# A three-pass feed-forward product with two token halves in one moving operand, and a join of smaller edits, in a one-core network kernel

## The chip, the cores and the metric

The kernel runs on one core of one Trainium2 chip. The metric is the device time of one execution in microseconds (us); the figure for a kernel is the median of several runs. A separate execution was taken by the hardware profiler; all rows below come from that one execution.

## The reference, cut to what matters

There are 256 tokens of width 1024, all in 32-bit floating point. The network is two blocks in a row:

```
h = x + 0.5 * rms_norm(swiglu(rms_norm(x), w_gate, w_up, w_down))      # ffn1
h = h + rms_norm(hybrid_mixer(rms_norm(h)) @ w_out)                    # mix
h = h + rms_norm(memory_cross_attention(rms_norm(h), rms_norm(mem)))   # mem
h = h + 0.5 * rms_norm(swiglu(rms_norm(h), ...))                       # ffn2
# second block, modulated by c @ w_ada + b_ada (six rows of 1024)
h = h + g1 * (conformer_conv + gated differential attention) @ w_out   # blk
h = h + g2 * mixture of 64 experts(norm(h))                            # moe

def swiglu(x, w_gate, w_up, w_down):
    return (silu(x @ w_gate) * (x @ w_up)) @ w_down                    # 1024 -> 2816 -> 1024
```

## The kernel before, in words

The stages ffn1, mix, mem, ffn2, blk and moe follow one another; each reads and updates the residual `h`, kept in the on-chip memory (SBUF) as two token tiles t = 0 and t = 1 of 128 tokens.

**Precision.** Most products are done in three passes. `split` (L178) cuts an operand into a high part `hi` (a cast by ACT to a 32-bit matmul type) and a low part `lo` (the rest, a subtraction on DVE); a product is hi·hi + hi·lo + lo·hi, three matmuls into one accumulator (`mm3`, L388; `lin_feat`, L573). Weights arrive from HBM in granules of 512 KB (`gran`, L294; four buffers `wraw`) and are split into `whi` and `wlo` (four buffers each).

**Feed-forward.** `ffn` (L527) does the first 512 of the 2816 inner columns in token-major form (`lin_tok2`, L434: the token slice is the stationary operand, 512 weight columns stream), and the remaining 2304 in nine blocks of 256 columns in feature-major form (`lin_feat`: a 128x128 weight block is stationary, all 256 tokens stream). In such a block each of the two matrices takes 8 slices of the inner dimension times 2 column groups times 3 matmuls:

```
583  nc.tensor.matmul(p, hi, xh[:, k], start=k == 0, stop=False)
584  nc.tensor.matmul(p, hi, xl[:, k], start=False, stop=False)
585  mm = nc.tensor.matmul(p, lo, xh[:, k], start=False, stop=k == K - 1)
```

After both matrices ACT takes silu of the gate sum out of the accumulator, DVE multiplies by the up sum, and the result is split into `hh`, `hl` (L554 to L558). The down projection (`lin_wide`, L464) uses token slices of these as stationary operands; its last eight slices are kept back and done for t = 0 first and then for t = 1, so that t = 0 is complete while t = 1 still runs.

**Between stages.** `post_norm` (L276) and `norm_T` (L226) finish the residual and make the next stage's normalised input: sums of squares on ACT, a power on POOL, products on DVE and POOL, then `trans` (L265), which transposes 4 slices at a time on the tensor engine (L186) and splits the result into two tensors `xTh` and `xTl` (`xT`, L193). For t = 0 the transposes come in program order, behind all matmuls of the stage before; for t = 1 they are kept in `second` and issued by `mid` (L254) behind a given matmul, the end of the first product's work on t = 0.

**Work hung between.** `tick` (L355) counts granules, and `at(n, f)` issues `f` at a later count. The modulation rows run this way inside the feed-forwards: 48 rounds of a DVE multiply-add of a 512 KB weight tile into `aacc` (L1337), and for each of the six rows `ada_end` (L1341), two matmuls with 32 columns of ones, a copy, and a store of one row to DRAM. Vectors that are wanted in all 128 partitions are loaded by `bcast` (L171) from one row in HBM; vectors that are wanted as columns go through `cols` (L588), a load of rows and a transpose.

Each engine does its instructions in the order in which the scheduler put them at build time; `issue_after(i)` places instructions behind `i` in the order of their engine. DMAs of weights are issued on SP's queue.

Of the kernel before, what the change touches and what calls it, by code (L numbers as in the profile page):

```python
# [26 lines left out]
CNORM = 1  # L27
# [92 lines left out]

def _freqs():
    import numpy as np

    return np.power(500000.0, -np.arange(0, 16, 2) / 16.0).astype(np.float32)[None]


class Net:


    def __init__(self, tc, A, es):  # L130
        self.tc, self.nc, self.A, self.es = tc, tc.nc, A, es
        pool = lambda name, bufs, **k: es.enter_context(tc.tile_pool(name=name, bufs=bufs, **k))
        self.cst = pool("cst", 1)
        self.wraw = pool("wraw", NRAW)
        self.whi = pool("whi", 4)
        self.wlo = pool("wlo", 4)
        self.act = pool("act", 1)
        self.ps = pool("ps", 8, space=PSUM)
        nc = self.nc
# [9 lines left out]
        self.now, self.todo, self.second, self.late = 0, [], [], []  # L149
        self.steady = {}  # L150
        self.tags, self.xp, self.half, self.xi, self.hold = None, None, None, 0, None
# [19 lines left out]
    def bcast(self, vec, n=D, tag="gB", bufs=3, eng=None):  # L171

        t = self.act.tile([P, n], F32, name=tag, tag=tag, bufs=bufs)
        (eng or self.nc.sync).dma_start(t, vec.broadcast_to([P, n]))
        return t
# [4 lines left out]
    def transpose_split(self, src, hi, lo, t, full=None):  # L180

        nc = self.nc
        n = src.shape[-1] // P
        pt = self.psum("tp")
        for c in range(n):
            nc.tensor.transpose(pt[:, c * P : (c + 1) * P], src[:, c * P : (c + 1) * P], self.ident)  # L186
        pv = pt[:, : n * P].rearrange("p (c t) -> p c t", c=n)
        sl = slice(t * P, (t + 1) * P)
        self.split(hi[:, :, sl], lo[:, :, sl], pv)
        if full is not None:  # L190
            self.nc.scalar.copy(full[:, :, sl], pv)

    def xT(self, tag="xT", bufs=1, kc=8):  # L193
# [32 lines left out]
    def norm_T(self, src, gain, pre=None, out=None, late=False):  # L226


        nc = self.nc
        gB = self.bcast(gain)  # L230
        hi, lo = out or self.xT()

        def tile(t):
            if pre is not None:
                pre(t)
            x = self.halves(src, t)
            rs = self.sumsq(x)
# [3 lines left out]
            nc.vector.tensor_scalar(xn[1], xn[1], rs, None, ALU.mult)  # L241
            for b in range(2):
                self.trans(xn[b], hi, lo, b, t)

        tile(0)
# [19 lines left out]
    def trans(self, xn, hi, lo, b, t, full=None):  # L265

        def tr():
            o = slice(4 * b, 4 * b + 4)
            self.transpose_split(xn, hi[:, o], lo[:, o], t, full if full is None else full[:, o])

        if t == 0:
            tr()
        else:
            self.second.append(tr)
# [19 lines left out]
    def gran(self, ap, eng=None, more=None):  # L294

        nc = self.nc
        kc, n = ap.shape[0] // P, ap.shape[1]
        raw = self.raw([P, kc, n])
        self.loaded = nc.sync.dma_start(raw, ap.rearrange("(c p) n -> p c n", p=P))
        return self.wsplit(raw, eng, more)  # L300

    def raw(self, shape):
# [6 lines left out]
        if tag != "wraw":  # L309

            if self.half is None:
                if tag == "xT":
                    self.xi = 1 - self.xi
                    x = self.act.tile([P, 2, 1024], F32, name="wx", tag="xTh" if self.xi else "xTl", bufs=1)
                else:
                    x = self.mp.tile([P, 2, 1024], F32, name="wx", tag=tag, bufs=LB)
# [117 lines left out]
    def lin_tok2(self, xT, blocks, more, done=None):  # L434
# [10 lines left out]
        for t in range(2):  # L445
            for i, ((W, c0, n, ps), hl) in enumerate(zip(blocks, ws)):
                for k, w in enumerate(hl):
                    x = [v[:, k, t * P : (t + 1) * P] for v in xT]
                    mm = self.mm3(ps[t][:, :n], x, w, k == 0, k == len(hl) - 1)
                    if t and k % 2:  # L450
                        self.tick(mm)
                if t and done is not None:
                    done(i)
            if t == 0:
                self.mid(mm)
# [8 lines left out]
    def lin_wide(self, xT, W, last=True, first=False, bias=None, ws=None, ps=None, more=None):  # L464
# [8 lines left out]
        def go(t, ws, n):  # L473
            for i, (k, hl) in enumerate(ws):
# [5 lines left out]
                if n and i % n == n - 1:  # L480
                    self.tick(mm)
            return mm

        k = 0
        while k < K:
# [7 lines left out]
            for t in range(2):  # L493
                mm = go(t, w, 2 if n > 1 else t)
                if k == t == 0:
                    self.mid(mm)
# [18 lines left out]
    def load_x(self):  # L515
# [3 lines left out]
        self.nc.sync.dma_start(self.ident, self.A["consts"][:, :P])  # L519

        def pre(t):
            if t == 1:
                self.nc.sync.dma_start(self.h[:, 1], x[:, 1])
# [3 lines left out]
    def ffn(self, n, pre=None, ada=()):  # L527
# [3 lines left out]
        with self.tc.tile_pool(name="ffn", bufs=1) as pool:  # L531
# [56 lines left out]
    def cols(self, rows, n, name="cols", dst=None, at=None, tag="ds"):  # L588

        nc = self.nc  # L590
        if at is None:
            r = self.act.tile([n, P], F32, name="rowsT", tag="rowsT", bufs=2)
        else:
            r = self.mp.tile([n, P], F32, name="rowsT", tag=tag, bufs={"ds": 3, "daT": 2}[tag])
        nc.sync.dma_start(r, rows)
        o = dst if dst is not None else self.mp.tile([P, n], F32, name=name)

        def turn():
            pt = self.psum("tp")
            nc.tensor.transpose(pt[:, :n], r, self.ident[:n, :n])  # L600
            nc.vector.tensor_copy(o, pt[:, :n])

        if at is None:
            turn()
        else:
            self.at(at, turn)
        return o
# [66 lines left out]
    def mixer_consts(self, mp):  # L674
# [10 lines left out]
        def loads():  # L685
# [5 lines left out]
            nc.sync.dma_start(gnB, A["gdn_out_norm"].broadcast_to([P, P]))  # L691
            for a, b, n in ((0, 1536, 8), (8, 3592, 8)):
# [5 lines left out]
        def tables():  # L698
            self.cols(A["gdn_conv_w"][0].rearrange("i (c p) -> (i c) p", p=P), 48, dst=cw)
# [610 lines left out]
    def ada_start(self):  # L1310
# [3 lines left out]
        self.modr = [dr.tile([1, D], F32, name="modr%d" % i) for i in range(6)]  # L1314
# [3 lines left out]
        def start():  # L1318
            self.cols(A["c_2"].rearrange("o (c p) -> (o c) p", p=P), 8, dst=self.cc)
# [21 lines left out]
    def ada_end(self, i, acc):  # L1341

        nc = self.nc
        ps = self.psum("ada")
        for b in range(2):
            nc.tensor.matmul(ps[32 * b : 32 * b + 32], self.ones[:, :32], acc[:, b * 512 : b * 512 + 512],
                             start=True, stop=True)
        r = self.mp.tile([P, 512], F32, name="ar", tag="s", bufs=3)[:64]
        nc.scalar.copy(r, ps[:64])
        for b in range(2):  # L1350
            nc.sync.dma_start(self.modr[i][:, b * 512 : b * 512 + 512], r[32 * b : 32 * b + 1])
# [26 lines left out]
    def norm_mod_T(self, gain, i, pre):  # L1378
# [6 lines left out]
        for t in range(2):  # L1385
# [76 lines left out]
    def conv_consts(self):  # L1462
        A = self.A
        row = lambda n: A[n].rearrange("o (c p) -> (o c) p", p=P)
        self.lng = self.cols(row("conv_ln_g_2"), 8, "lng", at=5, tag="daT")
        self.lnb = self.cols(row("conv_ln_b_2"), 8, "lnb", at=6, tag="daT")
        dw = A["conv_dw_2"][0].rearrange("i (c p) -> (i c) p", p=P)
        return [self.cols(dw[0:128], 128, "dw0", at=2), self.cols(dw[128:248], 120, "dw1", at=3),
                self.cols(row("conv_dw_b_2"), 8, "bdw", at=4)]
# [364 lines left out]
    def moe_norm(self, pre, each):  # L1834
# [4 lines left out]
        xf = self.act.tile([P, 8, T], F32, name="xf", tag="xTl", bufs=1)  # L1839
# [550 lines left out]
c_2 positions_2 w_ada_2 b_ada_2 norm1_g_2 w_in_2 conv_dw_2 conv_dw_b_2 conv_ln_g_2 conv_ln_b_2 w_pw2_2  # L2390
# [27 lines left out]
```

## Time and profile before

| What | Value |
|---|---|
| median of 3 runs | 1421.91 us (1420.5 to 1423.75) |
| the profiled execution's own time | 1420.49 us |
| its span, first to last instruction | 1418.7 us |
| PE (matmuls) busy | 1365.4 us, 96% |
| DVE busy | 902.9 us, 64% |
| ACT busy | 670.2 us, 47% |
| mean granted clock of the tensor engine | 0.995 of full |

PE is the tensor engine, DVE, ACT and POOL are the vector, scalar and general engines, SP issues the DMAs. Matmuls are pipelined: the duration in a row of PE contains the passage through the array, and what a matmul costs in a stream is the distance from one start to the next.

### The profile page before, as it was taken

The page shows a single profiled execution, that of the slowest core. Times are in us where ns is not written, and L with a number is a line of the kernel's source. Part 1 is how long each engine was busy: PE and PEld are TensorE (multiplying, and loading weights), DVE is VectorE, ACT ScalarE, POOL GpSimd, SP SyncE. Part 2 cuts the span into 40 slices and gives each one's busy share as a digit, 9 for nine tenths or more (in the row PEclk, how much of TensorE's full clock was granted, in tenths as well). Part 3 has the DMA queues.
Part 4 walks back from the last instruction along what each step waited for, and adds up shares of the span by engine and source line. Part 5 has one row for each costly group of instructions (what it writes and reads, how often), then busy time and mean ns, then how long its engine had stood idle before and what let it go on. Part 6 is the DMA issues. An engine that isn't in the chain of part 4 may idle for free.

```text
span 1418.7 us, 23583 instructions
## 1 busy us (share of the span) xinstructions
PE 1365.4 (96%) x8901; PEld 1068.5 (75%) x8901; DVE 902.9 (64%) x1419; ACT 670.2 (47%) x1055; POOL 127.5 (9%) x111
## 2 busy tenths in 40 slices
PE   6999999999999999999999989999999999999996
PEld 4999878889777879998798768675456566657662
DVE  5878567864457598664669997767226555555452
ACT  5544555634346454444453465943115444444440
POOL 1000012110101020000200313123000000000000
PEclk9999999999999999999999999999999999999999
DMA  8889666343245278875677534467889999999996
GB/s 283 272 291 321 208 197 211 102 137 107 75 158 180 94 262 303 280 241 182 199 242 214 168 119 134 134 209 280 336 317 409 408 408 354 409 408 409 365 409 260
DMA packets 148788, 358.00 MB, mean 252 GB/s; under 512 B 16099, under 2 KB 53931, under 8 KB 148671
## 3 DMA queue, kind: packets, MB, share of 16 engines
q1 hardware_dynamic: 148671, 356.46, 70.7%
q8 instruction: 71, 1.16, 0.3%
q14 instruction: 46, 0.38, 0.1%
HBM read 354.81 MB, written 1.60 MB: 251 GB/s over the span
## 4 chain that ended last, share of the span: by engine, by line
PE 44%; DMA 9%; DVE 7%; ACT 2%; issue 1%; POOL 0%; SPq 0%; DVEq 0%; ACTq 0%; POOLq 0%
DMA wx<-in_exp_gu 5%; PE eg L2209 4%; PE gx L2052 3%; DMA wx<-in_w_exp_down 3%; PE y L2220 2%; DVE wlo L178 2%; PE lw L393 2%; PE lw L392 2%; PE lw L391 2%; PE eg L2161 1%; PE eg L2160 1%; PE u L583 1%; PE g L584 1%; PE g L583 1%; PE u L585 1%
## 5 line engine op out<-in xcount | busy, mean ns | idle before, releaser
L178 DVE TENSOR_TENSOR wlo<-wraw,whi 128x1024 fp32r<-128x1024 f32 x248 | 308.9, 1253 | 137.5 <-ACT whi L178 135.6
L178 ACT CAST whi<-wraw 128x1024 fp32r<-128x1024 f32 x250 | 260.7, 1049 | 244.2 <-PE lw L393 50.1
L178 DVE TENSOR_TENSOR wlo<-wx,whi 128x1024 fp32r<-128x1024 f32 x76 | 89.8, 1221 | 18.7 <-ACT whi L178 17.7
L2209 PE MATMUL eg<-wx,xe 128*32 128x512 f32 (+1 forms) x480 | 84.1, 595 | 0.7 <-DMA wx<-in_exp_gu 0.7
L583 PE MATMUL u<-xTh,whi 128*128 128x256 f32 x288 | 82.2, 285 | 0.0
L583 PE MATMUL g<-xTh,whi 128*128 128x256 f32 x288 | 81.6, 283 | 0.0
L584 PE MATMUL g<-xTl,whi 128*128 128x256 f32 x288 | 81.5, 283 | 0.0
L585 PE MATMUL g<-xTh,wlo 128*128 128x256 f32 x288 | 81.5, 283 | 0.0
L585 PE MATMUL u<-xTh,wlo 128*128 128x256 f32 x288 | 81.5, 283 | 0.0
L584 PE MATMUL u<-xTl,whi 128*128 128x256 f32 x288 | 81.5, 283 | 0.0
L178 ACT CAST whi<-wx 128x1024 fp32r<-128x1024 f32 x76 | 77.0, 1050 | 8.0 <-DMA wx<-in_exp_gu 4.8
L2111 DVE SCALAR_TENSOR_TENSOR es<-es,gsl,eg 128x256 f32<-128x256 f32 (+2 forms) x27 | 13.0, 480 | 90.0 <-ACT es L2110 90.0
L1337 DVE SCALAR_TENSOR_TENSOR aacc<-wada,cc,aacc 128x1024 f32<-128x1024 f32 x48 | 61.5, 1282 | 9.9 <-DMA wada<-in_w_ada 9.5
L178 DVE TENSOR_TENSOR yl<-y,yh 128x512 fp32r<-128x512 f32 (+2 forms) x54 | 36.6, 688 | 43.8 <-ACT yh L178 43.8
L2110 ACT ACTIVATE es<-eg 128x256 f32<-128x256 f32 (+2 forms) x27 | 10.4, 384 | 111.2 <-PE eg L2209 90.8
L2209 PEld LDWEIGHTS eg<-wx,xe 128*32 128x32 f32 (+1 forms) x480 | 22.5, 116 | 48.3 <-issue 40.7
L2052 PE MATMUL gx<-G,h2h 128*128 128x256 f32 (+1 forms) x240 | 58.3, 285 | 0.0
L583 PEld LDWEIGHTS u<-xTh,whi 128*128 128x128 f32 x288 | 55.2, 192 | 3.4 <-ACT sf L556 3.4
L393 PE MATMUL lw<-whi,hl 128*128 128x512 f32 x144 | 56.8, 394 | 0.0
L391 PE MATMUL lw<-whi,hh 128*128 128x512 f32 x144 | 56.6, 393 | 0.0
L392 PE MATMUL lw<-wlo,hh 128*128 128x512 f32 x144 | 56.6, 393 | 0.0
L2052 PE MATMUL gx<-G,h2l 128*128 128x256 f32 (+1 forms) x240 | 56.6, 278 | 0.0
(698 smaller groups left out, 3689.9 us busy)
## 6 DMA issues: line engine op xcount, KB each, us to landing
wx<-in_exp_gu SPq DMA_DIRECT2D x172, 512.0 KB
wraw<-in_w_in SPq DMA_DIRECT2D x84, 512.0 KB
wx<-in_w_exp_down SPq DMA_DIRECT2D x84, 512.0 KB
wada<-in_w_ada SPq DMA_DIRECT2D x48, 512.0 KB
wraw<-in_ffn_w_gate SPq DMA_DIRECT2D x44, 512.0 KB
wraw<-in_ffn_w_up SPq DMA_DIRECT2D x44, 512.0 KB
wraw<-in_ffn_w_down SPq DMA_DIRECT2D x44, 512.0 KB
wraw<-in_exp_gu SPq DMA_DIRECT2D x40, 512.0 KB
```

The lines of the kernel that those rows point to most:

```text
L178: return self.nc.scalar.copy(hi, src), (eng or self.nc.vector).tensor_sub(lo, src, hi.bitcast(F32))
L391: nc.tensor.matmul(o, x[0], w[0], start=start, stop=False)
L392: nc.tensor.matmul(o, x[0], w[1], start=False, stop=False)
L393: return nc.tensor.matmul(o, x[1], w[0], start=False, stop=stop)
L583: nc.tensor.matmul(p, hi, xh[:, k], start=k == 0, stop=False)
L584: nc.tensor.matmul(p, hi, xl[:, k], start=False, stop=False)
L585: mm = nc.tensor.matmul(p, lo, xh[:, k], start=False, stop=k == K - 1)
L1337: nc.vector.scalar_tensor_tensor(acc, w, self.cc[:, k : k + 1], acc, ALU.mult, ALU.add)
L2052: nc.tensor.matmul(ps[:, i * n : (i + 1) * n], h[:, t, f], G[:, t], start=j == 0, stop=j == 3)
L2160: nc.tensor.matmul(ps, xh[:, c], hi, start=c == 0, stop=False)
L2209: mm = nc.tensor.matmul(ps[o], xe[:, k, o], w[k // 2][:, k % 2], start=k == 0, stop=k == 7)
L2220: mm = nc.tensor.matmul(y[o], hT[:, c, o], w[4 + c][:, 0, b * 512 : b * 512 + 512], start=c == 0, stop=c == 1)
```

## The change

Everything stands in one diff:

- In the nine feed-forward blocks `lin_feat2` takes the place of `lin_feat`. High and low token parts lie side by side, so that one matmul per high weight block streams 512 columns (high tokens into the left half of the accumulator, low tokens into the right), and the low weight block streams the 256 high columns into the left half. ACT then copies the right half out and DVE adds the left half to it, for gate and up, before the silu.
- The normalised input is held in two tiles of four slices each, with high and low inside a slice (`Half` gives the old view of it).
- `lin_wide` notes the matmul that ends its last slice but one for t = 1 (`gap`); the next stage's transposes for t = 0 are issued right behind it, at a raised priority. `mid` is called one or two slices earlier than before.
- In ffn1 the splits of the first four gate granules are placed behind steps of the first token tile's norm (`turns`). 18 matmuls of ones by ones are issued at the start (`WARM`). The first load of `x` is followed by the gain, then by the identity.
- Gains, the modulation rows and several column vectors lie in HBM already spread over 128 partitions or as columns; `cols` and its transposes go. `ada_end` does two matmuls with all 128 columns of ones and stores 128 rows.
- In the block's norm the product of the first half with the gain moves from POOL to DVE.

```diff
+class Half:
+    def __getitem__(self, key):
+        p, k, *rest = key
+        j = (k.start if type(k) is slice else k) // 4
+        k = slice(k.start - 4 * j, k.stop - 4 * j) if type(k) is slice else k - 4 * j
+        return self.tiles[j][(p, k, self.i, *rest)]
...
     def xT(self, tag="xT", bufs=1, kc=8):
-        hi = self.act.tile([P, kc, T], F32R, name=tag + "h", tag=tag + "h", bufs=bufs)
-        lo = self.act.tile([P, kc, T], F32R, name=tag + "l", tag=tag + "l", bufs=bufs)
-        return hi, lo
+        self.xw = [self.act.tile([P, kc // 2, 2, T], F32R, name=tag, tag=tag, bufs=2 * bufs) for _ in range(2)]
+        return [Half(self.xw, i) for i in range(2)]
...
+            self.turns = [first[0], first[1], first[1], first[2]]
...
         if t == 0:
-            tr()
+            with ExitStack() as es:
+                if self.gap is not None:
+                    es.enter_context(self.tc.issue_after(self.gap.ins))
+                    es.enter_context(self.tc.high_priority(offset=GAP))
+                done = tr()
...
+                if i == len(ws) - 2:
+                    if t and last and ws[-1][0] == K - 1:
+                        self.gap = mm
+                    if t == ws[0][0] == 0:
+                        self.mid(mm)
...
+        for _ in range(WARM):
+            self.nc.tensor.matmul(ps[:, :P], self.ones, self.ones, start=True, stop=True)
...
-                g, u = [self.psum_feat(n, FW // P) for n in "gu"]
-                self.lin_feat(xT, wg, c0, g)
-                self.lin_feat(xT, wu, c0, u)
+                g, u = [[self.psum(n) for _ in range(FW // P)] for n in "gu"]
+                self.lin_feat2(self.xw, wg, c0, g)
+                self.lin_feat2(self.xw, wu, c0, u)
                 for m in range(FW // P):
-                    s = pool.tile([P, T], F32, name="sf", tag="sf", bufs=4)
-                    nc.scalar.activation(s, g[m], AF.Silu)
-                    nc.vector.tensor_mul(s, s, u[m])
+                    s, v = [pool.tile([P, T], F32, name="sf", tag="sf", bufs=6) for _ in range(2)]
+                    for o, p in ((s, g[m]), (v, u[m])):
+                        nc.scalar.copy(o, p[:, T:])
+                        nc.vector.tensor_add(o, p[:, :T], o)
+                    nc.scalar.activation(s, s, AF.Silu)
+                    nc.vector.tensor_mul(s, s, v)
...
+    def lin_feat2(self, xw, W, c0, ps):
+                    both = lambda: nc.tensor.matmul(p.rearrange("p (i t) -> p i t", i=2), hi, xw[k // 4][:, k % 4],
+                                                    start=k == 0, stop=k == K - 1)
+                    if k < K - 1:
+                        both()
+                    mm = nc.tensor.matmul(p[:, :T], lo, xw[k // 4][:, k % 4, 0], start=False, stop=False)
+                    if k == K - 1:
+                        mm = both()
...
     def ada_end(self, i, acc):
-        ps = self.psum("ada")
         for b in range(2):
-            nc.tensor.matmul(ps[32 * b : 32 * b + 32], self.ones[:, :32], acc[:, b * 512 : b * 512 + 512],
-                             start=True, stop=True)
...
+            ps = self.psum("ada")
+            nc.tensor.matmul(ps, self.ones, acc[:, o], start=True, stop=True)
...
-                nc.gpsimd.tensor_mul(xn, x[b], gB[:, s])
+                (nc.gpsimd if b else nc.vector).tensor_mul(xn, x[b], gB[:, s])
```

## Rows read from the trace of the kernel before

**Rows 1.** The page: busy us (share) xcount; PE busy tenths in 40 slices.
```profile
PE 1365.4 (96%) x8901; PEld 1068.5 (75%) x8901; DVE 902.9 (64%) x1419; ACT 670.2 (47%) x1055; POOL 127.5 (9%) x111
...
PE   6999999999999999999999989999999999999996
```
**Rows 2.** Timeline of PE, one gate-and-up block: start us, us, instruction.
```profile
52.87 0.28 PE L583 MATMUL g<-xTh,whi 128*128 128x256 f32 x1
...
64.39 0.28 PE L583 MATMUL g<-xTh,whi 128*128 128x256 f32 x1
```
**Rows 3.** Timelines of PE and DVE, end of ffn1, start of mix.
```profile
203.63 0.40 PE L393 MATMUL lw<-whi,hl 128*128 128x512 f32 x1
...
206.97 0.48 DVE L241 TENSOR_SCALAR xn<-xn,rs 128x512 f32<-128x512 f32 x1
...
208.66 0.39 PE L391 MATMUL lw<-wmore,hh 128*128 128x512 f32 x1
...
210.03 1.04 PE L186 MATMUL tp<-ident,xn 128*128 128x128 f32 x8
211.54 0.50 PE L391 MATMUL fv<-whi,xTh 128*128 128x512 f32 x1 [0.47 <-ACT xTh L178]
```
**Rows 4.** The page, costliest groups: busy us, mean ns of one, idle before.
```profile
L557 DVE TENSOR_TENSOR sf<-sf,u 128x256 f32<-128x256 f32 x36 | 13.8, 418 | 2.2 <-PE u L585 2.2
```
**Rows 5.** Windows in the feed-forward blocks: busy us per engine, clock, DMA, GB/s.
```profile
52.90:145.00 92.10, 92.10 (x757) 89.97 (x756) 73.30 (x85) 43.53 (x66) 0.95 (x1) 1.00 0.91 309
...
532.50:626.70 94.20, 94.20 (x781) 93.18 (x781) 70.59 (x82) 42.98 (x64) 0.96 (x1) 1.00 0.86 285
```
**Rows 6.** Waits of DVE, 52.9 to 145: us in total, times, longest.
```profile
DVE wlo L178 <- ACT whi L178: 13.5, 16, 2.0
DVE aacc L1337 <- DMA wada<-in_w_ada: 2.4, 6, 0.6
```
**Rows 7.** Timeline of all engines, the first 28 us.
```profile
4.08 0.63 ACT L211 ACTIVATE junk<-h 128x512 f32<-128x512 f32 x1 [1.75 <-DMA h<-in_x]
...
8.87 1.26 POOL L239 TENSOR_TENSOR xn<-h,gB 128x512 f32<-128x512 f32 x1 [2.41 <-DMA gB<-in_ffn_pre_norm]
10.15 1.04 ACT L178 CAST whi<-wraw 128x1024 fp32r<-128x1024 f32 x1 [4.59 <-DMA wraw<-in_ffn_w_gate]
11.23 1.23 DVE L178 TENSOR_TENSOR wlo<-wraw,whi 128x1024 fp32r<-128x1024 f32 x1 [5.47 <-ACT whi L178]
11.49 1.04 ACT L178 CAST whi<-wraw 128x1024 fp32r<-128x1024 f32 x1 [0.30 <-DMA wraw<-in_ffn_w_gate]
12.37 0.75 DVE L240 SCALAR_TENSOR_TENSOR xn<-h,rs,gB 128x512 f32<-128x512 f32 x1
...
13.17 1.97 PE L186 MATMUL tp<-ident,xn 128*128 128x128 f32 x8 [13.17 <-DVE xn L240]
...
14.96 0.80 PE L391 MATMUL g<-whi,xTh 128*128 128x512 f32 x1
...
27.70 1.03 PE L186 MATMUL tp<-ident,xn 128*128 128x128 f32 x8
```
**Rows 8.** Waits of PE, whole span: us in total, times, longest.
```profile
PE lw L393 <- DVE xTl L178: 1.5, 1, 1.5
...
PE lw L391 <- ACT xTh L178: 1.0, 2, 0.8
```
**Rows 9.** Window of the block's join, columns as in rows 5.
```profile
940.00:946.00 6.00, 4.26 (x11) 3.16 (x12) 4.69 (x7) 0.72 (x2) 1.50 (x3) 0.72 0.79 223
```
**Rows 10.** Timelines and one group of PE: modulation row, whole-width plain 32-bit product, column transposes.
```profile
140.90 1.05 PE L1346 MATMUL ada<-aacc,ones 128*32 128x512 f32 x4
141.88 0.38 PE L583 MATMUL u<-xTh,whi 128*128 128x256 f32 x1
...
978.23 5.37 PE L2011 MATMUL sh<-wraw,xf 128*128 128x512 f32 x12
...
L600 PE MATMUL tp<-ident,rowsT x7: 222/225/272, 40.2 to 732.4; 8*128 8x8 f32 x4, 48*128 48x48 f32 x1, 128*128 128x128 f32 x1, 120*128 120x120 f32 x1
```

More of the change, by code (lines that the diff above doesn't have):

```diff
@@ L147, in __init__ @@
         self.h = self.cst.tile([P, 2, D], F32, name="h")
-        self.now, self.todo, self.second, self.late = 0, [], [], []
+        self.now, self.todo, self.second, self.late, self.turns, self.gap = 0, [], [], [], [], None
         self.steady = {}
-        self.tags, self.xp, self.half, self.xi, self.hold = None, None, None, 0, None
+        self.tags, self.xp, self.half, self.hold = None, None, None, None
     def low(self, n):
@@ L240, in tile @@
             nc.vector.scalar_tensor_tensor(xn[0], x[0], rs, gB[:, :512], ALU.mult, ALU.mult)
[L241 to L245, printed above, removed]
+            done = nc.vector.tensor_scalar(xn[1], xn[1], rs, None, ALU.mult)
+            return [(done,)] + [self.trans(xn[b], hi, lo, b, t) for b in range(2)]
+        first = tile(0)
         if late:
+            self.turns = [first[0], first[1], first[1], first[2]]
             self.late.append(lambda: tile(1))
@@ L268, in tr @@
             o = slice(4 * b, 4 * b + 4)
-            self.transpose_split(xn, hi[:, o], lo[:, o], t, full if full is None else full[:, o])
+            return self.transpose_split(xn, hi[:, o], lo[:, o], t, full if full is None else full[:, o])
         if t == 0:
-            tr()
-        else:
-            self.second.append(tr)
+            with ExitStack() as es:
[3 more added lines that the diff above has]
+                done = tr()
+            if b == 1:
+                self.gap = None
+            return done
+        self.second.append(tr)
     def post_norm(self, fps, gain, mul):
@@ L299, in gran @@
         self.loaded = nc.sync.dma_start(raw, ap.rearrange("(c p) n -> p c n", p=P))
-        return self.wsplit(raw, eng, more)
+        with ExitStack() as es:
+            for i in self.turns.pop(0) if self.turns else ():
+                es.enter_context(self.tc.issue_after(i.ins))
+            return self.wsplit(raw, eng, more)
     def raw(self, shape):
@@ L311, in raw @@
             if self.half is None:
[L312 to L316, printed above, removed]
+                pool, bufs = (self.act, 2) if tag == "xT" else (self.mp, LB)
+                x = pool.tile([P, 2, 1024], F32, name="wx", tag=tag, bufs=bufs)
                 self.half = x[:, 1]
@@ L586, in lin_feat @@
             self.tick(mm)
-    def cols(self, rows, n, name="cols", dst=None, at=None, tag="ds"):
+    def lin_feat2(self, xw, W, c0, ps):
         nc = self.nc
[L591 to L607, printed above, removed]
+        K, n = W.shape[0] // P, len(ps) * P
+        kc = 1024 // n
+        for k0 in range(0, K, kc):
+            for k, w in enumerate(self.gran(W[k0 * P : (k0 + kc) * P, c0 : c0 + n]), k0):
+                for m, p in enumerate(ps):
+                    hi, lo = [v[:, m * P : (m + 1) * P] for v in w]
+                    both = lambda: nc.tensor.matmul(p.rearrange("p (i t) -> p i t", i=2), hi, xw[k // 4][:, k % 4],
[5 more added lines that the diff above has]
+                        mm = both()
+            self.tick(mm)
     def b4(self, name, dtype=F32):
@@ L1313, in ada_start @@
         dr = self.es.enter_context(self.tc.tile_pool(name="dram", bufs=1, space=bass.MemoryType.DRAM))
-        self.modr = [dr.tile([1, D], F32, name="modr%d" % i) for i in range(6)]
+        self.modr = [dr.tile([P, D], F32, name="modr%d" % i) for i in range(6)]
         self.ud = [dr.tile([P, 2 * (T + 3)], F32, name="ud%d" % i) for i in range(2)]
@@ L1343, in ada_end @@
         nc = self.nc
-        ps = self.psum("ada")
         for b in range(2):
-            nc.tensor.matmul(ps[32 * b : 32 * b + 32], self.ones[:, :32], acc[:, b * 512 : b * 512 + 512],
-                             start=True, stop=True)
[L1348 to L1351, printed above, removed]
+            o = slice(b * 512, b * 512 + 512)
+            ps = self.psum("ada")
+            nc.tensor.matmul(ps, self.ones, acc[:, o], start=True, stop=True)
+            r = self.mp.tile([P, 512], F32, name="ar", tag="s", bufs=3)
+            nc.scalar.copy(r, ps)
+            nc.sync.dma_start(self.modr[i][:, o], r)
     def ada_jobs(self, rows, first, every):
@@ L1462, in conv_consts @@
     def conv_consts(self):
[L1463 to L1469, printed above, removed]
+        vc = self.mp.tile([P, 272], F32, name="vcols")
+        self.nc.sync.dma_start(vc, self.A["vcols"])
+        self.lng, self.lnb = vc[:, 256:264], vc[:, 264:272]
+        return vc[:, 0:128], vc[:, 128:248], vc[:, 248:256]
     def conv_in(self, xT, W, u, y, cw):
@@ L1838, in moe_norm @@
         tl = mp.tile([P, 2, D], F32R, name="h2l")
-        xf = self.act.tile([P, 8, T], F32, name="xf", tag="xTl", bufs=1)
+        xf = self.act.tile([P, 8, T], F32, name="xf", tag="xT", bufs=2)
         gB = self.mod_gain(A["norm2_g_2"], 4)
@@ L2409 @@
                     ("taps", _taps(np.asarray(inputs["conv_dw_2"])[0])),
+                    ("vcols", np.concatenate([_col(np.asarray(inputs[n])) for n in _COLS], 1)),
                     ("exp_gu", _pairs(np.asarray(inputs["w_exp_gu_2"])[0]))):
```

39 lines of the change are left out of this document (25 added, 14 removed).

## The prediction

> **What bounds the kernel now.** I read the page first. The tensor engine is busy for 96% of the span, and every slice but the first and the last stands at nine tenths or a hair under, while DVE has 64% and ACT 47% [rows 1]. So the end moves only by what PE itself has to do, by the few places where PE stands, and by whatever makes one of the other engines late enough to hold PE. A matmul's duration in a row holds its passage through the array; what it costs in a stream is the distance between starts. For 256 columns that distance comes out of one gate-and-up block: 96 matmuls from 52.87 to 64.39, 11.52 us, 0.120 us each [rows 2]. For 512 columns it comes out of the end of the down projection: 22 starts from 203.63 to 208.66, 5.03 us, 0.2286 us each [rows 3]. Next I read the windows of the two feed-forwards. In the first, DVE works 73.30 of 92.10 us and the DMA engines are 0.91 busy at 309 GB/s; in the second DVE works 70.59 of 94.20 [rows 5]. The list of waits says what DVE's 18.8 idle us are: 13.5 of them are waits for the high part of a weight granule from ACT, which itself waits for PE to free a buffer [rows 6], so they are slack, not a limit. Last come the first 28 us [rows 7] and PE's waits at the stage boundaries [rows 3, 8, 9].
>
> **The change part by part.** All against the profiled execution, 1420.49 us; the median of the runs stands 1.4 us above it.
>
> *The wide operand.* A slice and column group costs three 256-column matmuls now, 3 x 0.120 = 0.360 us, and will cost one of 512 and one of 256, 0.2286 + 0.120 = 0.3486. That saves 11.4 ns, and there are 576 such triples (2 feed-forwards x 9 blocks x 32): -6.6 us. The price of the 512-column form is read from token-major matmuls with another pattern of weights, so I bound it: no gain at all where the wide form costs twice the narrow one (0.240), -6.6 where it costs what rows 3 show. I take -6.
>
> One rule of the Trainium skill speaks against this term. "TensorE: Matmul & The Clock Gate", section "Back-to-back issue gap", gives an isolated gap of N/2.4 + 2.5 ns, so that nearly all of the price is columns. By it the triple would go from 327.5 to 325.0 ns, an estimate, and the term would be -1.4 us. The trace does not agree: the same two forms take 120 and 228.6 ns, with 11.4 ns that a merged matmul saves, and the section's sustained figure of about 131 ns for N=512 is further off still.
>
> *The hand-offs.* Each block gains four ACT copies and four DVE additions of 128x256. A DVE pass of that shape out of the accumulator takes 418 ns [rows 4], so DVE gets 1.67 us per block. At present it does 73.30 / 92.10 x 11.52 = 9.17 us per block, afterwards 10.84 of the 11.16 (32 x 0.3486) that PE would need: 97%. In the second feed-forward it is 8.63 + 1.67 = 10.30, 92%. DVE goes in order, and an addition stands behind a copy on ACT that stands behind the end of a column group; while it waits, the weight splits queue behind it on DVE, and PE waits for those. What covers it is the four buffers of split weights, about 1.4 us of PE work per granule. The lower bound of this cost is 0. The upper is DVE 10.84 us plus the idle that it does not lose to ACT now, (18.8 - 13.5) / 8 blocks = 0.66: 11.50, which is 0.34 per block above PE, x 9 for the first feed-forward, +3; with a hand-off exposed each time it would be more, and that is a rival. I take +3, the nearer row being the saturated first feed-forward. The accumulators are no limit: a tile already takes a whole bank's width of 512 and a block uses four of eight.
>
> *The start.* h lands by 4.08, but POOL stands until 8.87 for the gain, a single row spread by the DMA, and the first weight granule is there only at 10.15; the next follows at 11.49, 1.34 us for 512 KB [rows 7]. Between 4.08 and 10.15 two loads of 512 KB pass in 6.07 us, where 2 x 1.34 = 2.7 would do: 3.2 us to spare after the identity's small load. Besides, DVE splits the first weight at 11.23 (1.23 us) ahead of the norm's product at 12.37, which the first transposes at 13.17 wait for; the new order removes that. First matmul 14.96 now, about 10 after. The weights then arrive at 1.34 us per granule as before, so not all is kept: I put the end of the first set (27.70 now) at about 23. Bounds -2.5 (the granules set the pace) and -6.5 (both steps gained); I take -4.5. In the first stretch eight transposes take 1.97 us and later 1.03 [rows 7]: the first are at 1.2 GHz, the later at 2.4. The 18 early matmuls end before h's transposes can start and cost nothing if so; if they lift the clock, up to 1.3 us more is won. I take 0 for them.
>
> *The boundaries.* Now the transposes of t = 0 stand behind all of the last stage. In rows 3 they start at 210.03, the next product stalls 0.47 us for the split at 211.54, although the input xn ends at 207.45 (206.97 + 0.48), 1.2 us before the new place behind the matmul at 208.66. With the transposes there, ACT and DVE split while PE does the last slice, and the stall goes. The waits for xTh and xTl are ten rows of that list, 7.1 us in all, from 1.5 and 1.0 [rows 8] down to 0.2; about 0.5 of them belongs to the start, 6.6 stays. At the join into the second block PE's clock is 0.72 over 6 us [rows 9], so about 6 x 0.28 = 1.7 us is lost there beside the standing. Together 8.3. The block's norm product on DVE belongs here: it shortens the same chain for t = 1. What is late next is the second half's split and the wait for weights behind it, and not every xn is ready so early; if one is late, PE stands at the transposes with the last slice behind them. I take -7.5, bounds -11 (with some 0.2 us of refill per stall on top) and 0.
>
> *The modulation rows.* PE spends 0.98 us on such a row now (140.90 to 141.88, a 32-column product). With full columns the nearest row is the plain 32-bit product of 512 columns, 5.37 us for 12 records, 0.447 each, two per matmul [rows 10]: 2 x 2 x 0.447 = 1.79. So +0.8 x 6 = +4.9. Bounds 0 (the width of the weights is free) and +4.9. The stores grow from a row to 128, 2 x 256 KB per row on DMA engines at 0.91; that is 1.3 us of the transfer rate per row, which the ring of granules holds.
>
> *Transposes of columns.* Seven go, each 0.22 us in its row [rows 10], -1.5 if nothing of them overlaps and 0 if all does; I take -0.9.
>
> Sum: -6 + 3 - 4.5 - 7.5 + 4.9 - 0.9 = -11.0, so 1409.5 on the profiled execution and 1410 to 1411 as a median; I say 1410.
>
> **The rivals.**
>
> *A, the boundaries give nothing.* The early transposes stand in order on PE, and where xn or the splits come late they only move the wait. For it: most of these waits are for splits on ACT and DVE, which have weight splits queued. Against it: xn is 1.2 us early in rows 3. Then -3.5 is left: 1417 on the profiled execution, 1418 as a median.
>
> *B, slower: the hand-offs bind both feed-forwards.* DVE at 97% of a block has no room for a wait. If each block shows one exposed hand-off, the copy and the addition of two column groups (4 x 0.418 us of DVE plus as much idle), DVE needs 9.17 + 1.67 + 1.67 = 12.5 us per block, PE standing at the wlo of the next granule: +1.0 per block x 18 = +17.6 in place of -3. The sum is then 17.6 - 8.0 = +9.6, 1431 as a median. It decides from the point where the blocks lose 8.0 us in all, 0.45 each, a block of 11.97 us. For it: the 73.30 of rows 5. Against it: 13.5 of the idle in rows 6 is given back by PE, and the second feed-forward has room.
>
> *C, the wide matmul does not do what it says.* It costs twice the narrow one, or the merged pattern takes the fixed part back. The term is 0, the sum -5: 1415.5, 1417 as a median.
>
> **How the numbers follow.** Forecast 60%, A 18%, B 13%, C 9%. The likeliest gives 1410, with a range of its own of 1402 to 1417 from the bounds of its terms, since they will not all fall on one side. The whole range takes in A, C and break-even: 1400 to 1421, leaving out B and a few cases of everything going well. A change of 0.2% (2.8 us) is about what a measurement of this kernel can tell from none. Faster by more: nearly all of the forecast (0.58), half or more of A and C (0.17), 0.75. Within it: 0.11, the rest of A and C and a mild B. Slower: 0.14.
>
> **What would show it.** Right: blocks of about 11.2 us with starts of the wide form 0.229 apart; DVE near 87 us in the window of rows 5 with no PE wait for wlo; the first real matmul near 10 us; no wait for the splits behind a stage; 1.8 us per modulation row. Wrong: blocks above 11.97 with PE waiting on DVE, or the waits of rows 8 standing in new places, at the transposes; or a lower clock at the start and the join as before.

## The result, and the profile after

The changed kernel took 1404.12 us (median of 4 runs, 1403.18 to 1407.32) against 1422.26 for the kernel before beside it: ratio 0.9877, 95% interval 0.9861 to 0.9894. Forecast were 1410, faster, and 1400 to 1421. The profiled execution took 1404.64 us, its span 1402.8: 15.9 us less than in the profile of before, where the sum of the prediction was 11.0.

The page after, busy time and the tenths of PE and of its granted clock:

```profile
PE 1366.0 (97%) x8354; PEld 1045.7 (75%) x8354; DVE 922.7 (66%) x1486; ACT 693.1 (49%) x1131; POOL 124.1 (9%) x109
...
PE   8999999999999999999999989999999999999997
...
PEclk9999999999999999999999999999999999999999
```

PE is still the bound. Its first slice stands at 8 where it was 6 [rows 1], but 7.1 of its 35 us are the 18 early matmuls of ones, so this digit shows no gain. Without them PE's busy time is 6.5 us below that of before (1366.0 - 7.1 against 1365.4): of the 15.9 us about 6.5 are less busy time and about 9.4 less standing. Where the time went is read by setting equal instructions of the two traces side by side (start in us, before and after; worked out from the timelines of PE):

```
landmark                                  before    after   difference
first of the nine blocks, ffn1             40.38    36.88    -3.50
second block, ffn1                         52.87    48.87    -4.00
down projection of ffn1                   147.74   141.90    -5.84
small gate product of the mixer (gt)      235.86   229.10    -6.76
first of the nine blocks, ffn2            532.55   525.07    -7.48
down projection of ffn2                   639.41   630.20    -9.21
conformer product cb, first columns       717.08   707.65    -9.43
conformer product cb, second columns      741.32   730.69   -10.63
attention's means (muB)                   849.46   838.77   -10.69
gather of the experts (gx)                993.21   977.07   -16.14
last accumulation of the experts         1406.54  1391.66   -14.88
end of the span                          1418.7   1402.8    -15.9
```

So 3.5 us came at the start, 2.3 and 1.7 in the two loops over blocks, 1.2 within the conformer product, 5.5 between the attention and the experts, the rest mostly at the other boundaries; 1.3 was given back within the experts and 1.0 came behind them.

One gate-and-up block (timeline of PE) answers to rows 2, and the modulation row to rows 10:

```profile
60.08 0.39 PE L647 MATMUL g<-xT,whi 128*128 128x512 f32 x1
60.30 0.28 PE L651 MATMUL g<-xT,wlo 128*128 128x256 f32 x1
...
71.28 0.39 PE L647 MATMUL g<-xT,whi 128*128 128x512 f32 x1
...
134.54 1.88 PE L1394 MATMUL ada<-aacc,ones 128*128 128x512 f32 x4
135.86 0.79 PE L647 MATMUL u<-xT,whi 128*128 128x512 f32 x1
```

A block is 71.28 - 60.08 = 11.20 us long, where it was 11.52. The modulation row's four records start 0.43 us apart and the next matmul takes 0.79 instead of 0.40, so its time on PE is about 1.7 us.

Two windows of ffn1's loop answer to rows 5: the first ends ahead of the second modulation row, the second covers the stretch of rows 5. The wait of DVE for ACT, the same in both, answers to rows 6:

```profile
48.90:132.50 83.60, 83.60 (x474) 72.48 (x473) 76.85 (x109) 51.34 (x93) 0.95 (x1) 1.00 0.91 311
48.90:139.16 90.26, 90.26 (x506) 77.54 (x505) 81.44 (x115) 54.84 (x99) 0.95 (x1) 1.00 0.91 314
```

```profile
DVE wlo L212 <- ACT whi L212: 3.2, 4, 1.4
```

DVE is busy for 81.44 us, 90% of the stretch (73.30, 80%, before), its waits for ACT fell from 13.5 us to 3.2, and PE did not stand once: its busy time is the window's length.

The start, timeline of all engines, answers to rows 7:

```profile
1.08 7.08 PE L566 MATMUL warm<-ones 128*128 128x128 f32 x36 [1.08 <-POOL ones L178]
...
5.57 1.27 POOL L273 TENSOR_TENSOR xn<-h,gB 128x512 f32<-128x512 f32 x1 [2.76 <-DMA gB<-in_ffn_pre_norm]
...
7.38 0.75 DVE L274 SCALAR_TENSOR_TENSOR xn<-h,rs,gB 128x512 f32<-128x512 f32 x1 [1.71 <-POOL rs L237]
7.95 1.05 ACT L212 CAST whi<-wraw 128x1024 fp32r<-128x1024 f32 x1 [2.47 <-DMA wraw<-in_ffn_w_gate]
...
8.19 1.09 PE L220 MATMUL tp<-ident,xn 128*128 128x128 f32 x8
...
9.54 0.51 PE L433 MATMUL g<-whi,xT 128*128 128x512 f32 x1 [0.26 <-ACT xT L212]
...
23.54 1.04 PE L220 MATMUL tp<-ident,xn 128*128 128x128 f32 x8
```

The gain is used at 5.57 (8.87 before), the first weight at 7.95 (10.15), the first transposes start at 8.19 and take 1.09 us, as later ones do (13.17, and 1.97 us, the pace of half the clock), and the t = 1 transposes start at 23.54 (27.70).

The end of ffn1 answers to rows 3, the join before the experts (window, 6 us) to rows 9, and the list of PE's waits to rows 8:

```profile
203.38 1.04 PE L220 MATMUL tp<-ident,xn 128*128 128x128 f32 x8
204.17 0.48 PE L433 MATMUL lw<-wmore,hh 128*128 128x512 f32 x1
...
205.64 0.39 PE L433 MATMUL fv<-whi,xT 128*128 128x512 f32 x1
```

```profile
927.00:933.00 6.00, 6.00 (x29) 4.73 (x28) 5.83 (x8) 2.70 (x4) 1.59 (x1) 1.00 0.77 259
```

```profile
PE tp L220 <- DVE xn L1440: 1.2, 2, 0.9
...
PE tp L220 <- DVE xn L274: 0.9, 1, 0.9
...
PE g L433 <- ACT xT L212: 0.3, 1, 0.3
```

The transposes stand before the last slice, the next product follows without a stall, and at the join PE works for all of 6 us at a granted clock of 1.00, where it worked 4.26 at 0.72. Of the ten rows of waits for the transposed input (7.1 us) one is left, 0.3; in their place stand 2.1 us of waits for xn at the transposes (0.4 before, beside the 13.2 of the start).

### The profile page after: what moved, and what is told of

The parts are those of the page before. It is cut to its first block, busy times and chain, and to the rows that moved or that the text cites. A ratio compares the mean times of both kernels' runs of the same rounds, so it can differ in the third digit from the quotient of the medians.

```text
span 1402.8 us, 22616 instructions
## 1 busy us (share of the span) xinstructions
PE 1366.0 (97%) x8354; PEld 1045.7 (75%) x8354; DVE 922.7 (66%) x1486; ACT 693.1 (49%) x1131; POOL 124.1 (9%) x109
## 4 chain that ended last, share of the span: by engine, by line
PE 40%; DMA 10%; DVE 10%; ACT 2%; issue 2%; POOL 0%; SPq 0%; DVEq 0%; POOLq 0%; ACTq 0%
DMA wx<-in_exp_gu 5%; PE eg L2252 4%; DVE cy L1541 3%; PE gx L2095 3%; DVE wlo L212 3%; DMA wx<-in_w_exp_down 3%; PE u L647 2%; PE g L647 2%; PE y L2263 2%; PE lw L434 2%; PE lw L433 2%; PE lw L435 2%; PE eg L2204 1%; PE eg L2203 1%; PE g L651 1%
## 5 line engine op out<-in xcount | busy, mean ns | idle before, releaser
L647 PE MATMUL u<-xT,whi 128*128 128x512 f32 x288 | 104.4, 402 | 0.0
L647 PE MATMUL g<-xT,whi 128*128 128x512 f32 x288 | 102.0, 393 | 0.0
L651 PE MATMUL u<-xT,wlo 128*128 128x256 f32 x288 | 77.9, 281 | 0.0
L651 PE MATMUL g<-xT,wlo 128*128 128x256 f32 x288 | 77.8, 280 | 0.0
L2153 ACT ACTIVATE es<-eg 128x256 f32<-128x256 f32 (+2 forms) x27 | 10.4, 383 | 111.9 <-PE eg L2252 92.1
L647 PEld LDWEIGHTS u<-xT,whi 128*128 128x128 f32 x288 | 54.1, 188 | 12.2 <-ACT whi L212 1.0
L647 PEld LDWEIGHTS g<-xT,whi 128*128 128x128 f32 x288 | 54.0, 188 | 10.9
L651 PEld LDWEIGHTS u<-xT,wlo 128*128 128x128 f32 x288 | 54.4, 189 | 2.2 <-issue 1.0
```

What stands on the lines that cost most here:

```text
L647: both = lambda: nc.tensor.matmul(p.rearrange("p (i t) -> p i t", i=2), hi, xw[k // 4][:, k % 4], start=k == 0, stop=k == K - 1)
L651: mm = nc.tensor.matmul(p[:, :T], lo, xw[k // 4][:, k % 4, 0], start=False, stop=False)
```

## The experiments

All twelve are the changed kernel with one edit. Ratios are to the kernel before, run beside each; the changed kernel's own is 0.9877. The intervals are about 0.002 to 0.003 to either side, so differences under 3 or 4 us between two of these ratios are not resolved by the times, and for them the starts of equal instructions in the profiles are used ("late by" always means against the changed kernel).

**Gate and up back to three matmuls.**

```diff
-                self.lin_feat2(self.xw, wg, c0, g)
+                self.lin_feat(xT, wg, c0, g)
...
-                    for o, p in ((s, g[m]), (v, u[m])):
-                        nc.scalar.copy(o, p[:, T:])
-                        nc.vector.tensor_add(o, p[:, :T], o)
```

> The changed kernel with the gate-and-up blocks as before: three 256-column matmuls per triple, no copies and additions of halves. Theory T (the wide operand saves 11.4 ns per triple, and the hand-offs hide wholly behind PE): blocks of 11.52 us instead of 11.16, 18 x 0.36 = 6.5 us longer than the changed kernel, about 1410.5. Rival H (the hand-offs cost the 3 us that the prediction charged): 3 to 4 longer. Rival P (price nearly by columns alone): under 2 longer.

1409.45 us, 0.9918 (0.9902 to 0.9935). Late by 5.5 us at the last block of ffn2 (617.28 to 622.75), 6.2 in the attention, 4.2 at the end of the span. 17 blocks x 0.32 = 5.4: up to there the whole loss is PE's, and nothing came back for the hand-offs that went. H falls, and P too; the 6.5 of T was 5.8, since a block saves 0.32 and not 0.36.

**The hand-offs kept, the wide matmul split for six of eight slices.** The first and the last slice stay wide.

```diff
-                    both = lambda: nc.tensor.matmul(p.rearrange("p (i t) -> p i t", i=2), hi, xw[k // 4][:, k % 4],
-                                                    start=k == 0, stop=k == K - 1)
+                    both = lambda: ([nc.tensor.matmul(p[:, i * T : (i + 1) * T], hi, xw[k // 4][:, k % 4, i],
+                                                      start=False, stop=False) for i in range(2)][-1]
+                                    if 0 < k < K - 1 else
...
```

> The hand-offs stay (four copies and four additions per block), but for six of the eight slices the 512-column matmul is two of 256. T: the whole difference is PE's, 6/8 of 6.5 = 4.9 us longer, about 1409, blocks of 11.43 us. H: with blocks longer than before, DVE has more room, so part of the 4.9 is hidden by what the hand-offs cost already: 2 to 3 longer. P: under 1.5 longer.

1407.82 us, 0.9902 (0.9882 to 0.9922). Late by 3.6 us at the last block of ffn2, where 17 x 0.32 x 6/8 = 4.1 would be, 4.4 in the attention, 3.6 at the end. A block takes 11.44 us, which is 11.20 + 0.32 x 6/8: that is T with the measured block. H expected 2 to 3.

**Each addition of halves twice, then five times.**

```diff
+                        for _ in range(4):                                     # once in the first of the two
+                            d = pool.tile([P, T], F32, name="sd", tag="sd", bufs=2)
+                            nc.vector.tensor_add(d, p[:, :T], o)
                         nc.vector.tensor_add(o, p[:, :T], o)
```

> Each addition of a left and right half is done twice on DVE (one result is not used): 4 x 0.418 = 1.67 us of DVE more per block, 10.26 + 1.67 = 11.93 us for a block in which PE needs 11.16. T (DVE has some 0.9 us per block of room and no more): DVE binds, blocks lose up to 0.8 us, up to 14 us longer in all, 5 to 14 with what overlaps, and PE waits for wlo in the loop. Rival: DVE's durations overlap one another and the real room is wider: under 2 longer.

> Each addition of halves five times on DVE (four results not used). Start-to-start a 128x256 addition takes 0.33 us, a weight split 1.135. Per block DVE then has 4 x 1.135 + (8 + 16) x 0.33 = 12.46 us without any modulation round, PE needs 11.16. T (the room of e3 was elastic work, the modulation rounds, which the order puts off; behind them DVE binds): blocks of 12.5 us or more, 18 x 1.3 = 23 us longer than the changed kernel or more, 1427 and up, PE waiting on wlo; rival B of the prediction is then real, only further off. Rival (still hidden): under 3 longer.

Twice: 1403.35 us, 0.9871 (0.9855 to 0.9888): no loss. T as stated there falls. Groups of DVE in the same window of 83.6 us show why, first of the changed kernel, then of this one:

```profile
L1384 DVE SCALAR_TENSOR_TENSOR aacc<-wada,cc,aacc 128x1024 f32<-128x1024 f32 x18 | 23.1, 1282 | 1.6 <-DMA wada<-in_w_ada 1.5
```

```profile
48.90:132.50 83.60, 83.60 (x474) 72.43 (x473) 81.21 (x134) 51.02 (x92) 0.95 (x1) 1.00 0.92 310
...
L1386 DVE SCALAR_TENSOR_TENSOR aacc<-wada,cc,aacc 128x1024 f32<-128x1024 f32 x14 | 17.9, 1278 | 0.0
```

The count of modulation rounds fell from 18 to 14: the order written at build time put them off. Not all of them can go. A row takes 8 rounds, so the two rows whose matmuls fall into the loop need 16; by the second of these (134.54 and 134.44) 24 rounds were done in the changed kernel and 19 in this one (timelines of DVE). So up to 8 rounds, 8 x 1.28 = 10.3 us, can be put off without holding these matmuls, and 5 were. Besides, a 128x256 pass costs 0.33 us from start to start when others stand around it, not the 0.418 of its row, so the price of the hand-offs was 1.3 us per block and not 1.67 (timeline of DVE, changed kernel):

```profile
60.80 0.42 DVE L604 TENSOR_TENSOR sf<-u,sf 128x256 f32<-128x256 f32 x1
61.13 0.41 DVE L604 TENSOR_TENSOR sf<-g,sf 128x256 f32<-128x256 f32 x1
```

Five times: 1476.77 us, 1.0385 (1.0357 to 1.0413). The same window, one over the last eight blocks to the loop's end, and PE's waits from 48.9 to 200:

```profile
48.90:132.50 83.60, 69.31 (x345) 56.45 (x343) 75.21 (x159) 37.50 (x69) 0.96 (x1) 0.92 0.65 214
48.83:182.17 133.34, 107.74 (x522) 87.27 (x521) 119.92 (x240) 56.19 (x102) 0.96 (x1) 0.90 0.63 207
```

```profile
PE g L654 <- DVE wlo L212: 12.4, 5, 5.8
PE u L654 <- DVE wlo L212: 5.2, 4, 3.7
PE g L650 <- ACT whi L212: 5.1, 4, 1.9
PE u L650 <- ACT whi L212: 2.9, 3, 2.5
```

PE works 69.31 of 83.60 us, behind the weight splits on DVE; the clock falls to 0.92 and the loads to 214 GB/s. Rival B is a real mechanism, 73 us dear here rather than the 23 that the expectation worked out. Those 23 counted no modulation round, but 15 of them still fell into the eight blocks. DVE is busy there for 119.92 us, 26.9 more than the 93.03 that the same blocks take in the changed kernel (48.87 to 141.90). The rest of the 40.3 us by which they are longer is time in which DVE stands as well.

**The places of the transposes: both undone, then the early one of t = 0 alone.**

```diff
-                    if t and last and ws[-1][0] == K - 1:
-                        self.gap = mm                                          # both experiments
...
-                    if t == ws[0][0] == 0:
-                        self.mid(mm)                                           # the first alone, mid as before
```

> The early transposes at the stage boundaries undone: t = 0 in program order behind the stage before, and the late transposes issued where they were. T (the boundaries gave 7 to 9 us, over half of it at the join before the mixture of experts): 7 to 9 longer, 1411 to 1413, the waits for the transposed input back. Rival A of the prediction (the waits only move): under 2 longer. Rival: the mixture of experts, bound by its loads, takes half back: 3 to 5 longer at the end though 7 to 9 late before it.

> Only the early placing of t = 0's transposes is undone; the late ones stay at their earlier place. The places together gave 6.4 us before the mixture of experts. T (t = 0's stalls were the larger part): 3 to 5 us late at that stage, 3 to 6 longer at the end. Rival (the earlier place of the late transposes does it): under 2 longer.

Both: 1411.7 us, 0.9934 (0.9917 to 0.9950), late by 6.4 us before the experts and 4.7 at the end of the profiled span. Early place alone: 1409.28, 0.9918 (0.9901 to 0.9934), late by 7.0 before the experts (970.18 to 977.21) and 4.6 at the end. So what the traces show is t = 0's early place; the earlier place of the late transposes adds nothing there. By the medians the first kernel is 2.4 us longer than the second, which the intervals do not resolve. Of the 7.0, 1.1 had come by the conformer product (730.69 to 731.80) and 2.5 by the attention's means (838.77 to 841.28); at the experts' first product, behind the join, it is 7.3 (954.00 to 961.26). The join is thus the largest part, and the 1.4 of the attention may be that stage's own (see the last experiment). The waits for the transposed input and the low clock at the join are back (PE's waits, and the window answering to rows 9, of the second kernel):

```profile
PE lw L435 <- DVE xT L212: 1.4, 1, 1.4
...
PE lw L433 <- ACT xT L212: 0.7, 1, 0.7
```

```profile
934.00:940.00 6.00, 4.55 (x13) 3.50 (x13) 3.33 (x6) 0.00 (x0) 0.20 (x2) 0.72 0.79 205
```

**The start: no early matmuls, no order of the first splits, one gain as a row.** The edits take out the 18 matmuls; the line that sets `turns`; and the first gain from the list of vectors spread in HBM.

> The 18 early matmuls left out, all else as changed. T (they lift the clock before the transposes at 8.19 and cost nothing): the first transposes take about 2 us instead of 1.09 and the first products run at 1.2 GHz as before the change, start of the t = 1 transposes 1 to 2 us later than 23.54; 1 to 2 us longer. Rival (weights arrive at their own pace and bind the first set): within 0.7 of the changed kernel.

> The first four weight splits no longer placed behind steps of the norm. T: DVE splits a weight ahead of the norm's product again, the first transposes start up to 1.2 us later, 0.5 to 1.5 us longer. Rival: the order comes out the same since the weight now arrives after the input and the gain: no difference.

> Only the first gain is loaded as before, one row spread over 128 partitions. T (this load held up the queue for 3.2 us): the gain lands near 8.9 and the first weight near 10 again, the t = 1 transposes begin 2 to 3 us later than 23.54, 2 to 3 us longer. Rival (its order ahead of the identity was what mattered): under 1 longer.

Times: 1404.38 (0.9865, 0.9837 to 0.9892), 1405.16 (0.9873, 0.9845 to 0.9901), 1403.49 (0.9861, 0.9835 to 0.9887): none differs from the changed kernel. In the traces: without the early matmuls the first transposes take 1.97 us again, but the t = 1 transposes start at 23.34 (23.54): the early matmuls are worth nothing, as the rival has it, by which the weights bind the first set. Without the order DVE splits a weight first (8.88), the norm's product starts at 10.02 and the first transposes at 10.82 (7.38 and 8.19), and the t = 1 transposes come at 24.79, 1.25 late. With the gain from one row (timeline of POOL):

```profile
6.46 1.27 POOL L273 TENSOR_TENSOR xn<-h,gB 128x512 f32<-128x512 f32 x1 [3.65 <-DMA gB<-in_ffn_pre_norm]
```

it is used at 6.46 instead of 5.57, and the t = 1 transposes come 0.44 late. These are single profiles: in seven kernels of this document whose start and transposes were left alone, the changed one among them, the t = 1 transposes begin between 23.09 and 23.84, in one more (the paired rows with four loads) at 24.80. So the 0.44 is not told from that spread, and the 1.25 not with certainty. The row spread by the DMA was thus not what held the queue until 8.87; the rival, the order of the loads, remains: the gain now goes ahead of the identity. That order was not tried by itself.

**Modulation rows by the paired narrow product again**, read back by four loads, then with 128 rows stored by eight stores:

```diff
-                nc.tensor.matmul(ps, self.ones, acc[:, o], start=True, stop=True)
+            nc.tensor.matmul(ps[32 * b : 32 * b + 32], self.ones[:, :32], acc[:, b * 512 : b * 512 + 512], ...)
...
+                nc.sync.dma_start(self.modr[i][:, b * 512 : b * 512 + 512], r[32 * b : 32 * b + 32])
```

> Modulation rows by two products with 32 columns of ones again, started 0.007 us apart in the trace of before, 32 rows stored, and read back by four loads of 32 partitions. T (the full width costs PE 0.65 us per row more): 6 x 0.65 = 3.9 us shorter than the changed kernel at the end of the second feed-forward, 2 to 4 at the end of the span since the mixture of experts gives some back; about 1401. Rival (the four loads instead of one delay the block's norm or SP's queue): 1 us shorter to 3 longer.

> The paired 32-column products for the modulation rows, stored four times into the 128 rows, so that the block's loads are those of the changed kernel. T (0.55 to 0.65 us of PE per row): 3.3 to 3.9 us earlier at the end of the second feed-forward; with the block's order as in the changed kernel 2 to 4 shorter at the end, 1400 to 1402. Rival (the block's DVE and ACT order decides what is kept): no gain or a loss up to 3.

Four loads: 1407.34, 0.9887 (0.9860 to 0.9914). PE gained as T says: late by 1.3 us behind the start, it was 2.1 early where the block begins, 3.3 us over six rows. In the attention it lost 5: PE's waits there, of the changed kernel and of this one, are

```profile
PE dq L433 <- ACT whi L212: 2.9, 1, 2.9
...
PE dq L434 <- DVE wlo L212: 1.2, 1, 1.2
```

```profile
PE dq L435 <- ACT whi L214: 4.9, 1, 4.9
PE dq L436 <- DVE wlo L214: 3.3, 1, 3.3
```

Counted from the first conformer product, the softmax (its first dmx on DVE) starts at 114.2 us instead of 111.9, and the weight casts on ACT that follow are late with it; DVE's convolution steps stand in another order there (its last cy at 122.8 instead of 137.6), and what set that off was not isolated. Eight stores: 1406.25, 0.9905 (0.9875 to 0.9935). 0.76 early before the first down projection, then 2.8 late at its end: the norm's input came late and PE stood at the early transposes with the last slice behind them (PE's waits):

```profile
PE tp L220 <- DVE xn L274: 3.9, 3, 2.5
```

Here is rival A at one boundary, 2.5 us in one wait. Neither version beats the changed kernel.

**The block norm's product on POOL.**

```diff
-                (nc.gpsimd if b else nc.vector).tensor_mul(xn, x[b], gB[:, s])
+                nc.gpsimd.tensor_mul(xn, x[b], gB[:, s])
```

> The block norm's first product back on POOL (128x512 there 1.26 us, on DVE some 0.7). T (it shortens the chain to the second token tile's transposes by a POOL pass): PE's waits for xn at the block's start grow from 1.2 us by 1 to 2 us, 0.5 to 2 longer. Rival (the transposes wait for something else): within 0.7.

1405.1, 0.9888 (0.9869 to 0.9908). Only 0.3 late at the block's t = 1 transposes, so the mechanism of T is not seen; 2.9 late before the experts, nearly all of it behind the conformer product, where the kernel without early matmuls is 2.2 late as well though nothing near was changed. Inconclusive: the attention moves by 2 to 5 us from kernel to kernel, with the build-time order as the likely reason.

## Why the prediction was right, and what was mis-sized

- *Bound and direction* held: PE stayed the bound, and each gain is work or waiting that PE no longer has. The range alone proves little: it would have held the times of rivals A (1418) and C (1417) too. What tells them apart is the traces.
- *The wide operand*, -6 forecast: 18 x 0.32 = -5.8, shown from both sides by the first two experiments. The price by columns alone, -1.4, is out.
- *The hand-offs*, +3: the term that was most wrong; measured 0. The step that failed is the reading of DVE's 9.17 us per block as work that the block needs. A third of DVE's load in rows 5 was modulation rounds, and up to 8 of the 19, 10.3 of 24.4 us, could move (groups of DVE, 52.9 to 145, kernel before):

```profile
L1337 DVE SCALAR_TENSOR_TENSOR aacc<-wada,cc,aacc 128x1024 f32<-128x1024 f32 x19 | 24.4, 1282 | 2.5 <-DMA wada<-in_w_ada 2.4
```

  Rows counted at their duration instead of their distance made the additions dearer by a quarter: DVE should have had some 87 us in the window of rows 5 and had 81.44. The cover was also counted at half: a block has four granules (casts of whi at 60.72, 62.98, 65.87 and 68.57 in the block shown), so a granule is 2.8 us of PE work and not 1.4. B's break-even lay more than four extra passes per block away, and less than sixteen.
- *The modulation rows*, +4.9: a block with such a row is 1.72 us longer than the others now and was 1.16 longer before. The four rows in the loops give +0.46, +0.63, +0.56 and +0.56, about 0.55 x 6 = +3.3, and the paired experiment gave the same 3.3 back. The full-width price was right (1.79 forecast); the gap of 0.98 to the next matmul understated the old row, since the start ahead of it and that matmul's own successor each came another 0.1 late.
- *The start*, -4.5: -4.2 at the t = 1 transposes, which the forecast was about, and -3.5 by the first block, with parts that were not separated. The early matmuls give 0. The order of splits brings the first transposes 2.6 us forward, of which 1.25 was left at t = 1; the spread gain gave 0.4 there, and one profile of each does not settle either. The rest is left to the order of loads by elimination and was not tested.
- *The boundaries*, -7.5: 7.0 before the experts, from t = 0's place. The size came out closer than the parts: by rows 8 and 9 the join before the experts was to give 4.2 (2.5 of waits, 1.7 of clock) and gave 4.8, with the stalls and the low clock not separated; the boundaries ahead of the conformer product gave 1.1 of the 4.1 for all others; 1.4 appeared inside the attention.
- *Columns*, -0.9: too small. Between the two conformer rows of the table PE does the same 192 matmuls in both kernels; before, five column transposes stood among them, and the stretch was 1.20 us longer. One more, at 70.24, lengthened the block from 64.39 to 76.28 by 0.37. That is 1.6 for six, outside the forecast's bound of 1.5 for seven, since a row's 0.22 leaves out what the neighbours lose. The norm's product was not separated.

The sum by these is -5.8 - 3.5 + 3.3 - 7.0 - 1.6 = -14.6 of the -16.1 seen before the experts; the other 1.5 stays open. The profiled gain is 4.9 larger than the forecast's sum, and the hand-offs (3.0) and the modulation rows (1.6) are most of that. That the experts give back 1.3 is seen in other kernels too: 5.95 us late before them became 4.2 at the end in the first experiment, 7.0 became 4.6 in the one without t = 0's early place. The loads there move 382 GB/s over 400 us (DMA share 0.97), and PE's waits for loads shift with its arrival, but the listed waits, 1.8 us in all, are too few to carry all of it; the cause was not settled.

## What to carry to other kernels

Before charging new work on a busy engine, split its load into what the loop waits for and what is merely hung there, and price short passes by start-to-start distance: here DVE at 80% of the loop took 1.3 us per block more, and twice that, for nothing, but not five times that. Place the head of the next stage before the last slice of this one only as far as its input is ready: it gave up to 7 us here, and one late input cost 2.5. Gains of 1 to 3 us that pass through a stage whose order is made at build time are judged at landmarks before and behind it, not by the total.

## What the runs showed of the hardware that was not expected

Two 32-column products into different quarters of the accumulator start 0.007 us apart (140.901 and 140.908 in the trace of before) and share their time: the pair lengthens its block by 1.16 us, the full width by 1.72. A gain loaded from one row spread over 128 partitions was used only 0.9 us later than 128 rows of it (6.46 against 5.57, and 5.55 to 6.00 in the other kernels that load the 128 rows). And where PE was made to wait over a whole loop, as in the kernel with five additions, its granted clock fell to 0.92 in that window, and to 0.50 from 66.0 to 72.8, behind a wait of 1.9 us that ended at 65.78: there a wide matmul and its narrow one took 0.64 us together (68.04 to 68.68) instead of 0.35, so that the wait cost more than its own length.
